# Operand sums of a seven-product gate/up projection made by accumulating transfers

## The chip, the cores and the metric

The kernel runs on one core of one Trainium2 chip. The metric is device time in microseconds of one launch. A core has a matrix engine (PE), a vector engine (DVE), an activation engine (ACT), a general engine (POOL) and a synchronisation engine (SP); SP, ACT and POOL each issue transfers on a queue of their own. Every engine works through its own instructions in order and waits on semaphores of the others.

## The reference, cut to what matters

One decoder layer serves 1024 prompt tokens and 8 sample tokens with the same weights, so all of the work below has T = 1032 columns (tokens). After attention, pooling and memory branches are merged into `h`, the layer ends so:

```python
    x = x + h @ w['w_out'][l]
    gate, up = jnp.split(rmsnorm(x, w['ffn_norm_g'][l]) @ w['w_gate_up'][l], 2, axis=-1)
    return x + (jax.nn.silu(gate) * up) @ w['w_down'][l]
```

D_MODEL is 1024, the hidden width is 2816 (22 tiles of 128), all data is float32.

## The kernel before, in words

Everything lies transposed: 128 features on the partitions, tokens along the row. Each float32 operand of a product is split into a rounded high part (a copy on ACT, `split`, line 239) and the remainder (a subtraction on DVE, line 240), and a product is three matmuls: high x high, high x low, low x high.

The end of the layer has three stages. First the output projection: for n = 0 to 7 a `gemm` fills four column chunks of 258 tokens, and `ev` adds the residual (L1323, DVE), stores it, scales it by the norm gain into `y` (L1325, ACT), squares it (L1329, ACT) and adds the square to `ssq2` (L1330, POOL). The tiles `y` are the activations, `hn[0..7]`. Write Y1 and Y2 for the first and second 516 tokens, and a (n < 4) and b (n from 4) for the two halves of the features. The stage also forms the activation operands of the seven products, among them sums and differences of Y1a, Y2a, Y1b, Y2b: `T1` at n < 4, and at n >= 4 a chain of three POOL operations, L1344 to L1346, each using the result of the one before.

The second stage is the gate/up projection by a seven-product scheme (Strassen's, in Winograd's form). Two weight tiles of 128 outputs, each cut into two halves of the features, make a 2 x 2 block matrix a11, a12, a21, a22. `wcombos` loads them (L1367, L1368), makes four sums on POOL (L1372 to L1376) and splits seven weight operands (`combo`, "combos" 0 to 6 here). The split combos take turns in six buffers, three tags of two. `strassen` then runs products 0 to 6; each is 24 matmuls, twelve for each 258-token half (`ps[0]` and `ps[1]`), in PSUM banks of tags s, t, g, p. Product 0 is copied out by ACT as `p1` (L1400) and product 2 is accumulated on top of it in the same banks, so product 2 waits for both copies. DVE adds the rest together, and POOL multiplies by the norm factor `rstd2` (L1415, L1423, L1428). One `wcombos` and one `strassen` are called a set here. There are 22 sets, gate and up in turn for 11 pairs of tiles. The third stage is the down projection.

The order of the instructions on each engine, within what dependences allow, is set when the program is built, by a scheduler that plans with estimated costs. Buffers come from pools of fixed counts: `wr` (raw weights) two, `tS` (sums) four.

Of the kernel before, what the change touches and what calls it, by code (L numbers as in the profile page):

```python
# [193 lines left out]
def body(nc, tc, xT, memT, w_p, w_m, w_v, w_mk, w_mv, w_up, w_un, w_out, w_gu, w_dn, w_pool, w_cmp, gains, consts, jlt,  # L194
# [37 lines left out]
    def gv(n, i=0):  # L232
        return gn[:, _GW[n][0] + i:_GW[n][0] + i + 1]
# [1074 lines left out]
    def opsplit(t, src, w):  # L1308
        split(src, t[:, :w], t[:, w:2 * w])
        return t  # L1310

    hn = [None] * 8
    ssq2 = rstd
    B11, B21, B22, T1, T2o, T3, T4n = ([None] * 4 for _ in range(7))
    for oi, n in enumerate(range(8)):
        wh, wl = wload(w_out[n], 1024)
        yt = hn[n] = T2(name="y")

        def ev(ci, c0, w, ps):
            xr = mg(w)  # L1320
            SY.dma_start(xr, xT[n][:, c0:c0 + w])
            x1 = tmp2(w, name="x1")
            V.tensor_add(x1, ps, xr)  # L1323
            SY.dma_start(x1d[n][:, c0:c0 + w], x1)
            S.activation(yt[:, c0:c0 + w], x1, AF.Copy, scale=gv("ffn", n))  # L1325
            if oi == 0:
                S.activation(ssq2[:, c0:c0 + w], x1, AF.Square)
            else:
                S.activation(x1, x1, AF.Square)  # L1329
                G.tensor_add(ssq2[:, c0:c0 + w], ssq2[:, c0:c0 + w], x1)  # L1330

        gemm(wh, wl, hh_, hl_, KD, ev, "t", CH4)

        y1, y2 = yt[:, :HT], yt[:, HT:]
        if n < 4:
            B11[n] = opsplit(T2(F32R, "b11"), y1, HT)
            t = sp.tile([128, HT], F32, name="tL", tag="L", bufs=2)
            G.tensor_sub(t, y2, y1)
# [16 lines left out]

    cc = [0]

    def combo(src, w=512):
# [3 lines left out]
        return opsplit(t, src, w)  # L1362

    def wcombos(s1, s2):

        r1, r2 = ([wp.tile([128, 1024], F32, name="wr", tag="wr", padded_shape=[128, T]) for _ in range(2)])
# [12 lines left out]

    def product(ps, a, b, first=True):  # L1380
# [11 lines left out]
    def strassen(w, z1, z2):  # L1392

        q = lambda h, c: slice(h * HT + c * HC, h * HT + c * HC + HC)
        px, pr = two("st"), two("gp")
        p1, u2 = [], []
        product(px, w[0], B11)
        for c in range(2):
            p1.append(tmp2(HC, "p1"))
            S.copy(p1[c], px[c])  # L1400
        product(pr, w[1], T1)
        product(px, w[2], B21, False)
        for c in range(2):
            V.tensor_mul(z1[:, q(0, c)], px[c], rstd2[:, q(0, c)])
        pq = two("st")
        product(pq, w[3], B22)
        py = two("st")
        product(py, w[4], T2o)
        for c in range(2):
            u2.append(mg(HC))  # L1410
            V.tensor_add(u2[c], py[c], p1[c])
            u4 = tmp2(HC, "u4")
            V.tensor_add(u4, pr[c], u2[c])
            V.tensor_add(z1[:, q(1, c)], pq[c], u4)
# [8 lines left out]
        G.tensor_mul(z2[:, HT:], z2[:, HT:], rstd2[:, HT:])  # L1423
# [77 lines left out]
```

## Time and profile before

| | |
|---|---|
| time, median of 3 runs | 1869.57 us (1867.78 to 1874.47) |
| profiled execution, its own time | 1869.54 us |
| span of its trace | 1867.8 us |
| PE busy | 96% of the span |
| DVE, ACT, POOL busy | 65%, 47%, 39% |

The profile is one execution. Its time is 1.7 us more than the span of its trace. Times in the views count from the span's start. An engine is counted as busy from the start to the end of each instruction, and matmuls overlap, so a busy PE is not by itself PE at its best rate; the number of matmuls in a stretch tells more.

### The profile page before, as it was taken

What the parts mean: (1) busy time and instruction counts of PE and PEld (TensorE: products, weight loads), DVE (VectorE), ACT (ScalarE), POOL (GpSimd) and SP (SyncE); (2) the same over time, 40 slices, a digit from 0 to 9 for tenths busy, and PEclk for the clock granted to TensorE, in tenths of its full rate; (3) what the DMA queues carried; (4) which work ended last, traced back from release to release, by engine and by line L of the source; (5) the groups of instructions that cost most, each with busy time, mean ns of one, the idle gap of its engine ahead of it and who ended that gap; (6) DMA issues with size and microseconds to landing.
All of it is one profiled execution on the core that took longest, in us unless ns stands there. A gap on an engine that the chain in (4) does not pass through costs nothing.

```text
span 1867.8 us, 34509 instructions
## 1 busy us (share of the span) xinstructions
PE 1798.3 (96%) x12337; PEld 1729.2 (93%) x12337; DVE 1210.0 (65%) x2748; ACT 870.7 (47%) x2012; POOL 737.5 (39%) x865
## 2 busy tenths in 40 slices
PE   6999999999999999989999999999999999999999
PEld 5998998888988999979989998899999999999999
DVE  8875788663564766778886834866666666636332
ACT  5643766445454676657774545422322223314100
POOL 5300211556341645457753437655545545100000
PEclk9999999899999999989999999999999999999999
DMA  4243124999665111552325643122222222546122
GB/s 162 100 148 139 65 101 164 296 316 315 205 201 169 53 43 63 179 165 78 108 64 177 213 134 100 62 87 78 71 80 80 84 87 69 170 131 184 59 69 94
DMA packets 142366, 241.13 MB, mean 129 GB/s; under 512 B 21449, under 2 KB 100450, under 8 KB 142194
## 3 DMA queue, kind: packets, MB, share of 16 engines
q1 hardware_dynamic: 118722, 189.69, 31.2%
q0 software_dynamic: 8496, 30.23, 4.8%
q10 hardware_dynamic: 14976, 19.01, 2.9%
q8 instruction: 97, 1.59, 0.4%
q14 instruction: 75, 0.61, 0.1%
HBM read 176.31 MB, written 62.55 MB: 128 GB/s over the span
## 4 chain that ended last, share of the span: by engine, by line
PE 55%; DMA 5%; DVE 4%; issue 2%; ACT 2%; POOL 1%; SPq 0%; ACTq 0%; DVEq 0%; POOLq 0%
PE ps_t L257 10%; PE ps_s L1385 10%; PE ps_t L1385 9%; PE ps_g L257 7%; PE ps_s L257 7%; PE ps_p L1061 3%; PE ps_s L1032 3%; PE ps_t L1077 2%; PE ps_g L1385 2%; PE ps_p L1385 2%; DMA mg<-acd 1%; DMA mg<-gd 1%; DMA gt<-gd 1%; DMA olr<-od 1%; DVE t L240 0%
## 5 line engine op out<-in xcount | busy, mean ns | idle before, releaser
L257 PE MATMUL ps_g<-xh,wh 128*128 128x344 f32 x624 | 206.1, 330 | 3.9 <-ACT mg L543 2.3
L257 PE MATMUL ps_g<-xl,wh 128*128 128x344 f32 x624 | 201.7, 323 | 0.0
L257 PE MATMUL ps_g<-xh,wl 128*128 128x344 f32 x624 | 201.6, 323 | 0.0
L239 ACT CAST wh<-wr 128x512 fp32r<-128x512 f32 (+3 forms) x138 | 99.9, 746 | 199.9 <-PE ps_t L257 83.5
L1051 POOL TENSOR_SCALAR P<-P,st,gate 128x384 f32<-128x384 f32 (+2 forms) x192 | 125.6, 664 | 94.6 <-DVE st L1046 37.8
L240 DVE TENSOR_TENSOR wl<-wr,wh 128x512 fp32r<-128x512 f32 (+3 forms) x112 | 105.0, 946 | 56.9 <-ACT wh L239 55.5
L239 ACT CAST cw<-tS 128x512 fp32r<-128x512 f32 x88 | 54.3, 619 | 182.0 <-PE ps_t L1385 98.2
L522 ACT ACTIVATE P<-P,st 128x384 f32<-128x384 f32 (+2 forms) x192 | 112.1, 586 | 40.1 <-DVE st L519 36.3
L257 PEld LDWEIGHTS ps_g<-xh,wh 128*128 128x128 f32 x624 | 118.2, 189 | 9.2 <-ACT mg L543 4.1
L257 PEld LDWEIGHTS ps_g<-xl,wh 128*128 128x128 f32 x624 | 118.5, 190 | 1.1 <-issue 0.4
L257 PEld LDWEIGHTS ps_g<-xh,wl 128*128 128x128 f32 x624 | 118.2, 189 | 1.3 <-issue 0.2
L240 DVE TENSOR_TENSOR ptl<-ps_t,pth 128x512 fp32r<-128x512 f32 (+1 forms) x208 | 108.0, 530 | 15.6 <-ACT pth L239 13.4
L239 ACT CAST pth<-ps_t 128x512 fp32r<-128x512 f32 (+1 forms) x208 | 91.3, 457 | 46.6 <-PE ps_t L1077 29.2
L240 DVE TENSOR_TENSOR cw<-tS,cw 128x512 fp32r<-128x512 f32 x88 | 93.3, 1061 | 29.7 <-ACT cw L239 26.1
L1385 PE MATMUL ps_s<-t,cw 128*128 128x258 f32 x792 | 106.1, 283 | 3.1 <-ACT rq L274 3.1
L1385 PE MATMUL ps_t<-t,cw 128*128 128x258 f32 x792 | 106.8, 283 | 2.1 <-DVE t L240 2.1
L1385 PE MATMUL ps_s<-b,cw 128*128 128x258 f32 x792 | 107.8, 286 | 0.0
L1385 PE MATMUL ps_t<-b,cw 128*128 128x258 f32 x792 | 105.6, 282 | 0.3 <-issue 0.3
L1385 PEld LDWEIGHTS ps_s<-t,cw 128*128 128x128 f32 x792 | 100.0, 190 | 3.3 <-ACT rq L274 3.3
L1385 PEld LDWEIGHTS ps_t<-t,cw 128*128 128x128 f32 x792 | 99.6, 189 | 2.9 <-DVE t L240 2.9
L1385 PEld LDWEIGHTS ps_s<-b,cw 128*128 128x128 f32 x792 | 101.4, 192 | 0.3
L519 DVE CUSTOM_DVE_ANT_0 P<-ps_s,ct 128x384 f32<-128x384 f32 (+3 forms) x160 | 83.2, 530 | 27.0 <-PE ps_t L1077 18.1
(527 smaller groups left out, 5659.0 us busy)
## 6 DMA issues: line engine op xcount, KB each, us to landing
kpg<-pg_k SPq DMA_DIRECT2D x128, 192.0 KB, 4.1
wr<-w_gu SPq DMA_DIRECT2D x44, 512.0 KB, 3.8
gd<-mg ACTq DMA_DIRECT2D x72, 172.0 KB, 3.4
wr<-w_m POOLq DMA_DIRECT2D x24, 512.0 KB, 5.4
acd<-zu SPq DMA_DIRECT2D x44, 258.0 KB, 2.0
mg<-acd SPq DMA_DIRECT2D x66, 172.0 KB, 3.0
mg<-gd SPq DMA_DIRECT2D x48, 172.0 KB, 2.4
wr<-w_p SPq DMA_DIRECT2D x16, 512.0 KB, 3.4
```

What stands on the lines that cost most here:

```text
L239: (he or S.copy)(hi, src)
L240: (le or V.tensor_sub)(lo, src, f(hi))
L257: PE.matmul(ps, lhsT=x, rhs=y, start=i == 0, stop=i == n - 1)
L519: V.tensor_tensor_reduce(P[u], s, m, -scale, ini, ALU.add, ALU.min, st[:, u:u + 1])
L522: S.activation(P[u], P[u], AF.Exp, bias=nm, scale=-1.0, accum_out=st[:, 6 + u:7 + u])
L1032: PE.matmul(ps, lhsT=u["q"][:, i * 128:i * 128 + 128], rhs=kk[:, k0 * 128 + a:k0 * 128 + a + n], start=x == 0, stop=x == 1)
L1051: lastp[:] = [G.tensor_scalar(p_, p_, st4[:, j, 5:6], gate[:, q, c:c + 1], op0=ALU.mult, op1=ALU.mult)]
L1061: PE.matmul(pv[:, c0:c0 + n], lhsT=lh, rhs=rhs, start=pvs["n"] == 0, stop=last, skip_group_check=True)
L1077: PE.transpose(pt_[:, x * 128:x * 128 + 128], pd[y][:, o - offs[y]:o - offs[y] + 128], ident)
L1385: PE.matmul(ps[c], lhsT=a[:, x * 512 + k * 128:x * 512 + k * 128 + 128], rhs=b[k][:, y * HT + c * HC:y * HT + c * HC + HC], start=first an ...
```

## The change

The sums of weights and the chain at n >= 4 are no longer computed on POOL. Each is a transfer that adds its source to its destination (`acc`), issued on POOL's queue, so POOL no longer computes in the last stages and only issues. A transfer can add but not subtract, so signs are moved: some activations are scaled by the negative gain (`ngn`), the raw tile r1 is negated in place on ACT (L1391 after), and some splits negate (`nsplit`). The weight tile's blocks are loaded several times, once into each sum's buffer. `x1` is one buffer that is added to three times and split between (combos 1, 3 and 4). The raw tile `wr` is now used once for each set, and `tS` has six buffers. Squares and the products with `rstd2` go to DVE, as do `T1` and all low parts. The products with `T2o` and `B22` change places.

```diff
+    def nsplit(src, hi, lo):
+        S.activation(hi, src, AF.Copy, scale=-1.0)
+        V.scalar_tensor_tensor(lo, src, -1.0, f(hi), op0=ALU.mult, op1=ALU.subtract)
+
+    def acc(dst, src):
+        G.dma_start(dst, src, accum_op=ALU.add)
...
-            S.activation(yt[:, c0:c0 + w], x1, AF.Copy, scale=gv("ffn", n))
+            S.activation(yt[:, c0:c0 + w], x1, AF.Copy,
+                         scale=gv("ffn", n) if (ci < 2) == (n < 4) else ngn[:, n:n + 1])
...
-                G.tensor_add(ssq2[:, c0:c0 + w], ssq2[:, c0:c0 + w], x1)
+                V.tensor_add(ssq2[:, c0:c0 + w], ssq2[:, c0:c0 + w], x1)
...
-            G.tensor_sub(x2, y2, x2)
-            G.tensor_add(x1, x1, x2)
-            G.tensor_sub(y1, y1, x1)
+            acc(x2, y2)
+            acc(x1, x2)
+            acc(y1, x1)
...
-        SY.dma_start(r1, s1)
-        SY.dma_start(r2, s2)
-        a11, a12, a21, a22 = r1[:, :512], r1[:, 512:], r2[:, :512], r2[:, 512:]
-        tS = lambda: sp.tile([128, 512], F32, name="tS", tag="S", bufs=4)
-        x1, x2, x3, x4 = tS(), tS(), tS(), tS()
-        G.tensor_add(x1, a21, a22)
-        r = [combo(a11), combo(x1), combo(a12)]
-        G.tensor_sub(x2, x1, a11)
-        G.tensor_sub(x4, a12, x2)
-        G.tensor_sub(x3, a11, a21)
-        r += [combo(x4), combo(x2), combo(x3), combo(a22)]
+        n11, n12 = r1[:, :512], r1[:, 512:]
+        SY.dma_start(r1, s1)
+        SY.dma_start(x1, s2[:, :512])
+        SY.dma_start(x3, s2[:, :512])
+        SY.dma_start(a22, s2[:, 512:])
+        acc(x1, s2[:, 512:])
+        S.activation(r1, r1, AF.Copy, scale=-1.0)
+        r = [combo(n11, True), combo(x1, True), combo(n12)]
+        acc(x1, n11)
+        acc(x3, n11)
+        r.append(combo(x1))
+        acc(x1, n12)
+        r += [combo(x1, True), combo(x3, True), combo(a22, True)]
...
-        G.tensor_mul(z1[:, HT:], z1[:, HT:], rstd2[:, HT:])
+        V.tensor_mul(z1[:, HT:], z1[:, HT:], rstd2[:, HT:])
...
-            split(src, t[:, :HT], t[:, HT:], le=G.tensor_sub if nm in ("t3", "t4") and k % 2 else None)
+            split(src, t[:, :HT], t[:, HT:])
```

POOL's queue before, at the end of the first stage (n = 7; `y_14234` is hn[3], `y_14816` hn[7], `wr` and `tS` those of the second set):

```order
L1344 TENSOR_TENSOR y_14234<-y_14816,y_14234 128x516
L1345 TENSOR_TENSOR y_14234<-y_14234 128x516
L1346 TENSOR_TENSOR y_14816<-y_14816,y_14234 128x516
L1330 TENSOR_TENSOR rstd_155<-rstd_155,x1_14943 128x258
L240 TENSOR_TENSOR t3_15078<-y_13940,t3_15078 128x516
L240 TENSOR_TENSOR t3_15084<-y_14234,t3_15084 128x516
L240 TENSOR_TENSOR t4_15090<-y_14526,t4_15090 128x516
L240 TENSOR_TENSOR t4_15096<-y_14816,t4_15096 128x516
L1372 TENSOR_TENSOR tS_15312<-wr_15309 128x512
```

The same place after (`y_14236` is hn[3], `y_14818` hn[7], `tS_15021` is x1 of the first set, `tS_15312` of the second):

```order
L1324 DMA tS_15021<-wr_15020 128x512
L1324 DMA y_14089<-y_14089 128x516
L1324 DMA y_14673<-y_14089 128x516
L1324 DMA y_14236<-y_14818 128x516
L1324 DMA tS_15021<-wr_15020 128x512
L1324 DMA y_14236<-y_14236 128x516
L1324 DMA y_14818<-y_14236 128x516
L1324 DMA tS_15560<-wr_15558 128x512
```

Computing instructions have become transfers, and a sum of the first set's weights now stands between the first and the second step of the last chain.

PE's queue before, around the first use of operands that need the chain (tiles b11, t1, b22 and t2 are activation operands, `rstd` with `ones` is the sum of squares over features):

```order
L1385 MATMUL ps_p_15104<-t1_14372,cw_15030 128x258 x3
L1385 MATMUL ps_t_15184<-b22_15051,cw_15039 128x258 x3
L1385 MATMUL ps_t_15184<-b22_15054,cw_15039 128x258 x3
L1385 MATMUL ps_t_15184<-b22_15057,cw_15039 128x258 x3
L1385 MATMUL ps_t_15184<-b22_15060,cw_15039 128x258 x3
L1385 MATMUL ps_t_15210<-t2_15063,cw_15042 128x258 x3
L1385 MATMUL ps_t_15210<-t2_15066,cw_15042 128x258 x3
L1385 MATMUL ps_t_15210<-t2_15069,cw_15042 128x258 x3
L1385 MATMUL ps_t_15210<-t2_15072,cw_15042 128x258
L1353 MATMUL ps_s_14986<-rstd_155,ones_141 128x258
L1385 MATMUL ps_s_15101<-b11_13926,cw_15027 128x258 x3
```

And after:

```order
L1405 MATMUL ps_t_15187<-t2_15054,cw_15041 128x258 x2
L1368 MATMUL ps_s_14988<-rstd_155,ones_141 128x258
L1405 MATMUL ps_s_15104<-b11_13928,cw_15030 128x258 x3
L1405 MATMUL ps_s_15104<-b11_14075,cw_15030 128x258 x3
L1405 MATMUL ps_s_15104<-b11_14222,cw_15030 128x258 x3
L1405 MATMUL ps_s_15104<-b11_14369,cw_15030 128x258 x3
L1405 MATMUL ps_t_15187<-t2_15054,cw_15041 128x258
L1405 MATMUL ps_t_15187<-t2_15057,cw_15041 128x258
L1405 MATMUL ps_s_15186<-t2_15054,cw_15041 128x258 x3
L1405 MATMUL ps_s_15186<-t2_15057,cw_15041 128x258 x3
L1405 MATMUL ps_s_15186<-t2_15060,cw_15041 128x258 x3
```

The T2o product, whose last tile needs two steps of the chain at n = 7, has moved ahead of the B22 product, which needs none, and product 2 (b21) has moved behind both.

ACT's queue before, for one gate or up set in the middle of the stage (weights of `wr_16050`, `wr_16051`):

```order
L239 CAST cw_16059<-wr_16050 128x512
L239 CAST cw_16062<-tS_16054 128x512
L239 CAST cw_16065<-wr_16050 128x512
L239 CAST cw_16071<-tS_16057 128x512
L239 CAST cw_16074<-tS_16055 128x512
L239 CAST cw_16077<-tS_16056 128x512
L1400 COPY p1_16121<-ps_s_16093 128x258
L239 CAST cw_16080<-wr_16051 128x512
L1400 COPY p1_16123<-ps_t_16094 128x258
```

And after, the set with `wr_16056` (`tS_16057` is x1, `wr_16554` the raw tile of the set after next):

```order
L1320 ACTIVATE cw_16066<-wr_16056 128x512
L1320 ACTIVATE cw_16069<-tS_16057 128x512
L239 CAST cw_16072<-wr_16056 128x512
L239 CAST cw_16077<-tS_16057 128x512
L1320 ACTIVATE cw_16081<-tS_16057 128x512
L1320 ACTIVATE cw_16084<-tS_16058 128x512
L1420 COPY p1_16128<-ps_s_16100 128x258
L1391 ACTIVATE wr_16554<-wr_16554 128x1024
L1320 ACTIVATE cw_16087<-tS_16059 128x512
L1420 COPY p1_16130<-ps_t_16101 128x258
```

Combos 1, 3 and 4 now read one buffer, and the negation of a later set's raw tile stands between the two copies of product 0.

## Rows read from the trace of the kernel before

**Rows 1.** The page, first part: busy time of each engine, its share, instructions.
```profile
PE 1798.3 (96%) x12337; PEld 1729.2 (93%) x12337; DVE 1210.0 (65%) x2748; ACT 870.7 (47%) x2012; POOL 737.5 (39%) x865
```

**Rows 2.** Windows in the seven-product stage; times x instructions, then granted clock, DMA share.
```profile
core 0: us, PE busy (x) PEld busy (x) DVE busy (x) ACT busy (x) POOL busy (x), PEclk, DMA share, GB/s
...
1200.00:1300.00 100.00, 100.00 (x839) 100.00 (x839) 67.84 (x116) 29.09 (x53) 53.67 (x36) 1.00 0.24 85
...
1500.00:1600.00 100.00, 100.00 (x839) 100.00 (x838) 64.71 (x112) 31.16 (x56) 52.72 (x35) 1.00 0.21 72
```

**Rows 3.** Timeline of PE, 1148 to 1200 us: start, duration, instruction, idle before it.
```profile
1156.48 0.28 PE L257 MATMUL ps_t<-mh,wl 128*128 128x258 f32 x1
...
1166.96 0.62 PE L1385 MATMUL ps_t<-t,cw 128*128 128x258 f32 x3 [0.90 <-DVE t L240]
...
1178.16 2.25 PE L1385 MATMUL ps_s<-t,cw 128*128 128x258 f32 x12 [3.12 <-ACT rq L274]
...
1189.94 1.62 PE L1385 MATMUL ps_s<-b,cw 128*128 128x258 f32 x12
```

**Rows 4.** Timeline of POOL, the last operand sums and splits ahead of the products.
```profile
1163.04 1.61 POOL L1344 TENSOR_TENSOR y<-y 128x516 f32<-128x516 f32 x1 [0.70 <-ACT y L1325]
...
1166.43 1.62 POOL L1346 TENSOR_TENSOR y<-y 128x516 f32<-128x516 f32 x1
...
1169.06 6.85 POOL L240 TENSOR_TENSOR t<-y,t 128x516 fp32r<-128x516 f32 x4
```

**Rows 5.** Timeline of DVE, then ACT, same stretch.
```profile
1168.86 7.60 DVE L240 TENSOR_TENSOR t<-y,t 128x516 fp32r<-128x516 f32 x5
...
1177.63 0.48 ACT L274 ACTIVATE rq<-ps_s,epst 128x258 f32<-128x258 f32 x1 [3.28 <-DVE rq L273]
```

**Rows 6.** Groups by line and form, 1190 to 1610 us: busy, mean ns, idle before.
```profile
L240 DVE TENSOR_TENSOR cw<-tS,cw 128x512 fp32r<-128x512 f32 x82 | 87.1, 1063 | 29.0 <-ACT cw L239 25.4 <-POOL zg L1428 3.2
...
L239 ACT CAST cw<-tS 128x512 fp32r<-128x512 f32 x81 | 50.2, 619 | 177.7 <-PE ps_t L1385 98.2 <-POOL tS L1372 66.9 <-POOL tS L1376 6.7
...
L1376 POOL TENSOR_TENSOR tS<-wr 128x512 f32<-128x512 f32 x20 | 34.9, 1745 | 0.0
...
L1450 DVE TENSOR_TENSOR zu<-zu,zg 128x516 f32<-128x516 f32 x41 | 28.5, 696 | 12.3 <-POOL zu L1428 11.9
...
L1413 DVE TENSOR_TENSOR u<-ps_g,mg 128x258 f32<-128x258 f32 x21 | 9.0, 427 | 0.7
...
L1400 ACT COPY p<-ps_s 128x258 f32<-128x258 f32 x21 | 7.8, 373 | 10.8 <-PE ps_s L1385 10.8
```

**Rows 7.** Tile wr and line L1285 (ns min/median/max); timeline of ACT, one cast of 1024 columns.
```profile
L240 DVE TENSOR_TENSOR cw<-wr,cw x61: 684/693/1781, 1195.1 to 1595.6; 128x512 fp32r<-128x512 f32 x61
...
L1285 DVE SCALAR_TENSOR_TENSOR ml<-acc,mh x24: 504/518/1244, 1021.9 to 1068.1; 128x344 fp32r<-128x344 f32 x24
...
1135.51 1.03 ACT L239 CAST wh<-wr 128x1024 fp32r<-128x1024 f32 x1
```

**Rows 8.** DMA issues: out<-in, queue, count, KB each, median us from issue to landing.
```profile
wr<-w_gu SPq DMA_DIRECT2D x44, 512.0 KB, 3.8
...
wr<-w_m POOLq DMA_DIRECT2D x24, 512.0 KB, 5.4
...
wr<-w_up POOLq DMA_DIRECT2D x8, 512.0 KB, 4.1
...
ol<-osp POOLq DMA_DIRECT2D x8, 256.0 KB, 2.4
...
ct<-consts POOLq DMA_DIRECT2D x1, 782.5 KB, 8.7
```

**Rows 9.** Line L244, instructions that issue a transfer on POOL: ns min/median/max.
```profile
L244 POOL DMA_DIRECT2D wr<-w_m x24: 538/557/610, 258.2 to 718.8; - x24
```

**Rows 10.** Timeline of PE, 1500 to 1521 us.
```profile
1500.05 1.62 PE L1385 MATMUL ps_s<-b,cw 128*128 128x258 f32 x12
...
1517.23 1.61 PE L1385 MATMUL ps_s<-b,cw 128*128 128x258 f32 x12
```

More of the change, by code (lines that the diff above doesn't have):

```diff
@@ L1310, in opsplit @@
         return t
+    ngn = sp.tile([128, 8], F32, name="ngn", tag="ngn", bufs=1)
+    V.tensor_scalar(ngn, gn[:, _GW["ffn"][0]:_GW["ffn"][0] + 8], -1.0, None, op0=ALU.mult)
+    def nsplit(src, hi, lo):
[3 more added lines that the diff above has]
+        G.dma_start(dst, src, accum_op=ALU.add)
     hn = [None] * 8
@@ L1336, in body @@
             B11[n] = opsplit(T2(F32R, "b11"), y1, HT)
-            t = sp.tile([128, HT], F32, name="tL", tag="L", bufs=2)
-            G.tensor_sub(t, y2, y1)
+            t = sp.tile([128, HT], F32, name="tL", tag="S", bufs=6)
+            V.tensor_add(t, y1, y2)
             T1[n] = opsplit(T2(F32R, "t1"), t, HT)
@@ L1356, in body, with combo @@
     cc = [0]
-    def combo(src, w=512):
+    def combo(src, neg=False):
         tag = ("wh", "wl", "wx")[cc[0] % 3]
@@ L1361, in combo @@
         t = (sp if tag == "wx" else wp).tile([128, 1024], F32R, name="cw", tag=tag, bufs=2)
-        return opsplit(t, src, w)
+        (nsplit if neg else split)(src, t[:, :512], t[:, 512:])
+        return t
     def wcombos(s1, s2):
-        r1, r2 = ([wp.tile([128, 1024], F32, name="wr", tag="wr", padded_shape=[128, T]) for _ in range(2)])
+        tS = lambda: sp.tile([128, HT], F32, name="tS", tag="S", bufs=6)[:, :512]
+        r1 = wp.tile([128, 1024], F32, name="wr", tag="wr", padded_shape=[128, T])
+        x1, x3, a22 = tS(), tS(), tS()
+        n11, n12 = r1[:, :512], r1[:, 512:]
         SY.dma_start(r1, s1)
-        SY.dma_start(r2, s2)
-        a11, a12, a21, a22 = r1[:, :512], r1[:, 512:], r2[:, :512], r2[:, 512:]
-        tS = lambda: sp.tile([128, 512], F32, name="tS", tag="S", bufs=4)
-        x1, x2, x3, x4 = tS(), tS(), tS(), tS()
-        G.tensor_add(x1, a21, a22)
-        r = [combo(a11), combo(x1), combo(a12)]
-        G.tensor_sub(x2, x1, a11)
-        G.tensor_sub(x4, a12, x2)
-        G.tensor_sub(x3, a11, a21)
-        r += [combo(x4), combo(x2), combo(x3), combo(a22)]
+        SY.dma_start(x1, s2[:, :512])
[9 more added lines that the diff above has]
+        r += [combo(x1, True), combo(x3, True), combo(a22, True)]
         return r
@@ L1404, in strassen @@
             V.tensor_mul(z1[:, q(0, c)], px[c], rstd2[:, q(0, c)])
-        pq = two("st")
-        product(pq, w[3], B22)
         py = two("st")
-        product(py, w[4], T2o)
+        product(py, w[3], T2o)
+        u4 = []
         for c in range(2):
@@ L1411, in strassen @@
             V.tensor_add(u2[c], py[c], p1[c])
-            u4 = tmp2(HC, "u4")
-            V.tensor_add(u4, pr[c], u2[c])
-            V.tensor_add(z1[:, q(1, c)], pq[c], u4)
-        G.tensor_mul(z1[:, HT:], z1[:, HT:], rstd2[:, HT:])
+            u4.append(tmp2(HC, "u4"))
+            V.tensor_add(u4[c], pr[c], u2[c])
+        pq = two("st")
+        product(pq, w[4], B22)
+        for c in range(2):
+            V.tensor_add(z1[:, q(1, c)], pq[c], u4[c])
+        V.tensor_mul(z1[:, HT:], z1[:, HT:], rstd2[:, HT:])
         pz = two("st")
@@ L1422, in strassen @@
             V.tensor_add(z2[:, q(1, c)], pr[c], u3[c])
-        G.tensor_mul(z2[:, HT:], z2[:, HT:], rstd2[:, HT:])
+        V.tensor_mul(z2[:, HT:], z2[:, HT:], rstd2[:, HT:])
         pw = two("st")
@@ L1427, in strassen @@
             V.tensor_add(z2[:, q(0, c)], pw[c], u3[c])
-        G.tensor_mul(z2[:, :HT], z2[:, :HT], rstd2[:, :HT])
+        V.tensor_mul(z2[:, :HT], z2[:, :HT], rstd2[:, :HT])
     acd = [dp.tile([128, T], F32, name=f"acd{i}") for i in range(NFF)]
     w = wcombos(w_gu[0], w_gu[1])
-    for o, nm, at, h in ((B22, "b22", 4, 1), (T2o, "t2", 0, 0), (T3, "t3", 0, 1), (T4n, "t4", 4, 0)):
+    for o, nm, at, h in ((T2o, "t2", 0, 0), (B22, "b22", 4, 1), (T3, "t3", 0, 1), (T4n, "t4", 4, 0)):
         for k in range(4):
             t, src = XG(nm), hn[at + k][:, h * HT:h * HT + HT]
-            split(src, t[:, :HT], t[:, HT:], le=G.tensor_sub if nm in ("t3", "t4") and k % 2 else None)
+            split(src, t[:, :HT], t[:, HT:])
             o[k] = t
```

## The prediction

> **What bounds the kernel now.** I read the page's first part, then the seven-product stage in windows, then the places where PE waits. PE is busy 96% of the span and every other engine at most 65% [rows 1], so only time in which PE stands still or runs slowly can be won. In the seven-product stage there is none: PE is busy for all of each window, at full granted clock, with 839 matmuls in 100 us [rows 2]. That is 0.1193 us for one matmul, 2.86 us for a product of 24 and 20.0 us for a set of seven. POOL is busy 53% there and DVE 65 to 68% [rows 2], and neither stops PE. So nothing that makes POOL or DVE cheaper in this stage can shorten it by itself.
>
> The place to win is the passage from the output projection to the first set. The last matmul of the projection starts at 1156.48 and lasts 0.28, so it ends at E = 1156.8; the second set starts at 1189.94 [rows 3]. The first set thus takes 33.2 us where its 168 matmuls need 20.0. Four sums of squares over the features lie between them, but most of the rest, some 11 to 12 us, is waiting. PE's timeline names the waits: DVE's split of an operand, then ACT's logarithm for the norm [rows 3]. ACT in turn waits 3.28 us for DVE [rows 5]. DVE is late because five of its splits take 7.60 us, or 1.5 each [rows 5], while POOL does four of its own in 6.85 [rows 4]; a split alone takes 0.69 [rows 7].
>
> **What the change removes.** On POOL, in each set four sums (the dearest 1.75 us [rows 6]) and three products, and ahead of the first set the chain, 1163.04 to 1168.05 for n = 7 [rows 4]. What POOL had cost DVE goes too: the split of a sum takes 1063 ns on average [rows 6] against a median of 693 for a split of raw weights [rows 7].
>
> **What it adds on DVE and ACT.** DVE gets three products of 516 columns in each set, at about 0.70 (L1450, same shape [rows 6]), together 2.1 us; four faster splits give back 4 x 0.37 = 1.5. The new form that negates and subtracts has the price of a plain subtraction: it took 518 ns for 344 columns [rows 7], and a straight line from 427 ns for 258 columns [rows 6] to 693 for 512 [rows 7] gives 517. DVE stays near 70%. ACT gets a negation of 1024 columns, 1.03 us [rows 7], and goes from 31% [rows 2] to 36%. The cover of both is PE's 20.0 us a set; neither becomes the bound.
>
> **What it adds on the transfers.** Four accumulating transfers in each set, 88 in all, and twelve for the activations. Their price D, from the moment the issue may start to the moment the next user may go on, is the unknown that decides. The trace has no accumulating transfer and none from SBUF to SBUF. The cheapest of POOL's queue with the same 256 KB takes 2.4 us; with 512 KB they take 4.1 and 5.4, with 782 KB 8.7 [rows 8]. An accumulating transfer reads its destination as well as its source, so it reads 512 KB, and I take the 512 KB row from the quieter stretch, D = 4.1, with 2.4 and 8.7 as the ends. The issue itself is 0.56 us of POOL [rows 9], hardly any load.
>
> **The first set, step by step.** After E, ACT still has a weight split (0.62 [rows 6]) and the last chunk of y (at most as much) to do, so y is ready at about E + 1.3. The T2o product needs hn[3] after two steps of the chain, one behind the other: E + 1.3 + 2D. Behind its split, ACT has, in the new order, four splits for B22, eight for T3 and T4 less one, and a weight: 13 casts at 0.62 are 8.1 us. Then come the copies of product 0 (0.37 [rows 6]), and product 2, T3 and T4 cannot start before them: 3 x 2.86 = 8.6. DVE's half of the same splits, 13 x 0.69, runs just behind and is covered. The second set starts at E + 1.3 + 2D + 8.1 + 0.4 + 8.6 = E + 18.4 + 2D. At D = 4.1 that is E + 26.6 against E + 33.2: 6.6 us won. The floor is the matmuls themselves, E + 20.0 and the four sums of squares; the gain is gone at D = 7.4. The other sum of the first set that stands in the chain's way on POOL's queue waits for a weight split that ends by E + 2.5, before the second step can start anyway.
>
> The Trainium skill, DMA: Bandwidth & Descriptors, Anatomy of one DMA, gives a transfer from POOL's queue as 2.0 us plus its bytes at 436 GB/s. That estimate is 3.2 us for 512 KB, and by it this passage would win 8.4 us and the whole would take 1861.1 us. The rows of 4.1 and 5.4 [rows 8] are slower than that estimate of the Trainium skill, and I follow the rows.
>
> **The later sets.** Here each set has a new chain, which must fit under PE. There are six buffers for seven split operands, so combo 1 of a set can be written when product 2 of the set before is done. In the trace, product 3 of a set starts at 1500.05 and product 2 of the next at 1517.23 [rows 10]: 17.2 us, six products. In that time x1 is split (0.62 + 0.69), added to (D), split again (1.31) and added to again (D). Only then is raw buffer r1 free; ACT's new order places the negation of the next load of that buffer between the two copies of product 0. So a load (3.8 [rows 8]), the negation (1.03), a split (0.62) and the copy (0.37) follow, and product 2's second half, which starts 1.43 later than the first, waits for the last of these. The chain is 2D + 8.4, to which I add two of DVE's evacuations queued ahead of the splits, 0.43 each [rows 6]: 2D + 9.3. The room is 17.2 + 1.4 = 18.6. At D = 4.1 the chain takes 17.5 and is hidden, with 1.1 us to spare; above D = 4.65 each set loses 2(D - 4.65), 21 times. What waits then is the copy p1 on ACT, and behind it PE.
>
> **The sum.** The profiled execution took 1869.54, which is the median of the three runs (1869.57), its span 1867.8 with 1.7 around it. 1869.5 - 6.6 + 0 = 1862.9, 0.4% less. I call anything within 0.5%, or 9.3 us, the same, about what a measurement of this kernel can tell from no change.
>
> **The rivals.**
> (1) Late operands: D is above 4.65 and every set stalls. For it speaks that POOL's 512 KB loads took 5.4 us in the busier stretch [rows 8], that the transfers per set rise from 1.3 MB to well over 2, and that the price of an accumulation is unseen; against it the quieter row of 4.1. At D = 5.4 the passage wins 33.2 - 29.2 = 4.0, and the sets lose 21 x 1.5 = 31.5: 1897. At the far end, D = 8.7, the passage loses 2.6 and the sets 21 x 8.1 = 170: 2042. It decides against the change by over 9.3 us from D = 4.65 + (9.3 + 5) / 42 = 5.0. Chance 0.35 for that.
> (2) A cheap transfer: D is near the 256 KB row, 2.4 [rows 8]. The first set then takes 23.2 us and 10.0 are won: 1859.5. To win over 9.3 us takes D below 2.75. For it speaks that the destination lies in SBUF and the row is the same size; against it the second read. Chance 0.15.
> (3) POOL cannot write its transfers' descriptors while DVE works. The issue takes 538 to 610 ns, in stretches where DVE was half busy [rows 9], and does not stretch, so little speaks for it. If each issue waited for two instructions of DVE (0.69 each), D would be 5.5 and the time 21 x 1.7 - 3.8 = 32 above, 1901. Chance 0.04. The Trainium skill, SBUF — State Buffer, Who interferes with whom, has such a lock for vector instructions that use both port pairs, and says that sums of two tensors are not among those that block the descriptors.
> (4) The passage is not shortened: another wait, the norm's logarithm or the copies queued on ACT behind the T2o split, keeps PE where it was, and the sets hide their chains. 1869, inside the forecast's class.
>
> **How the numbers follow.** Forecast, D from 2.75 to 4.65 with the sets hidden, 1860 to 1865: 0.36. Rival 4 and small stalls, D up to 5.0, 1865 to 1879: 0.10. Rival 2: 0.15. Rivals 1 and 3: 0.39. So faster by over 0.5% has 0.15, same 0.46, slower 0.39. The likeliest single case is the forecast, 1863, own range 1859 to 1867. The range for all goes from 1857, where the passage wins nearly the 13.2 us that the matmuls allow, to 1905, which takes in D up to about 5.6 and leaves out the dearest transfers, some 0.15.
>
> **What would show it.** Right: the accumulating transfers land 3.5 to 4.6 us after their issue; the second set starts about 27 us after the projection's last matmul; DVE's splits all take 0.69; PE has 838 matmuls in every 100 us of the later sets. Wrong: PE waits at product 2 in every set, with ACT's copy as the releaser and the negation waiting for a load, which is rival 1; a transfer that lands in time but is issued late behind another on POOL's queue; the first T2o product waiting beyond E + 12; or POOL's issues stretched above 0.7 us, which is rival 3.

## The result and the profile after

The changed kernel takes 1881.95 us (median of 7 runs, 1876.43 to 1886.02) against 1872.43 of the kernel before (7 runs, 1867.78 to 1874.47). The ratio is 1.0052, with a 95% interval of 1.0037 to 1.0067: slower, by 9.5 us at the medians. The profiled execution of the changed kernel took 1884.72 us, its span 1882.8.

First the windows of the changed kernel, as in [rows 2].

```profile
core 0: us, PE busy (x) PEld busy (x) DVE busy (x) ACT busy (x) POOL busy (x), PEclk, DMA share, GB/s
1200.00:1300.00 100.00, 96.73 (x793) 96.31 (x792) 62.96 (x123) 34.57 (x60) 17.57 (x20) 0.98 0.58 143
1500.00:1600.00 100.00, 100.00 (x837) 100.00 (x836) 67.06 (x131) 33.40 (x58) 15.80 (x18) 1.00 0.53 134
```

The later sets are as good as before (837 matmuls against 839), but the window from 1200 has 46 matmuls fewer. PE's waits from 1050 to 1640 us say where (us in total, times, the longest):

```profile
PE ps_t L257 <- DVE x L1337: 4.4, 5, 1.8
PE ps_t L1405 <- ACT p L1420: 2.8, 1, 2.8
PE ps_s L1405 <- ACT t L239: 2.5, 1, 2.5
```

L1337 is the evacuation of the output projection (the step that takes a finished chunk out of PSUM). The second row is one wait of the third set, the third the passage's. Before, PE waited 1.0 us for the evacuation there:

```profile
PE ps_t L257 <- DVE x L1323: 1.0, 2, 0.6
```

So the stretch is read in four parts. In the table, "projection" runs from the first matmul of the output projection to the end E of its last, "passage" from E to the start of the second set, then come the sets 2 to 5 (from the start of the second to the start of the fifth) and the rest to the end of the last matmul of the 22nd. All are read from PE's timeline as in [rows 3]; where the start of a set is split into pieces, it is that of its product 1 less 2.86. x3 is the buffer of the third weight operand; the kernels below are described with the experiments. The two profiles of before differ by 1.4 and 0.8 us in the first two columns, so smaller differences there say nothing. Each ratio is to runs of the kernel before that were taken together with that kernel.

| us, one profiled execution each | projection | passage | sets 2 to 5 | rest | time, median | ratio to before (95%) |
|---|---|---|---|---|---|---|
| before | 95.8 | 33.2 | 60.3 | 361.9 | 1872.43 | |
| before, a second profile | 94.4 | 32.4 | 60.3 | 361.9 | | |
| the change | 100.7 | 30.4 | 65.7 | 362.6 | 1881.95 | 1.0052 (1.0037 to 1.0067) |
| squares elsewhere | 96.2 | 29.3 | 63.5 | 362.4 | 1873.44 | 1.0011 (0.9998 to 1.0024) |
| squares on POOL | 103.4 | 34.4 | 65.7 | 362.7 | 1884.62 | 1.0072 (1.0045 to 1.0098) |
| no x3 sum (work left out) | 100.2 | 29.9 | 60.4 | 362.6 | 1874.35 | 1.0007 (0.999 to 1.0025) |
| weights only | 101.5 | 32.0 | 64.3 | 362.4 | 1881.36 | 1.0077 (1.0057 to 1.0097) |
| x3 last | 93.7 | 27.2 | 65.0 | 362.4 | 1866.17 | 0.9981 (0.9967 to 0.9996) |
| queues ordered | 94.2 | 25.0 | 65.1 | 362.4 | 1865.46 | 0.9976 (0.9964 to 0.9988) |
| x3 on DVE | 94.3 | 29.3 | 61.4 | 362.7 | 1865.75 | 0.9977 (0.9964 to 0.999) |
| x3 on POOL | 93.9 | 27.4 | 63.1 | 362.8 | 1865.92 | 0.9976 (0.9961 to 0.999) |
| last y first | 93.9 | 27.4 | 65.0 | 362.4 | 1867.34 | 0.998 (0.9968 to 0.9992) |
| ordered, no x3 (work left out) | 94.2 | 27.9 | 61.5 | 362.8 | 1866.21 | 0.9971 (0.9951 to 0.9991) |

Against the mean of the two profiles of before, the change loses 5.6 us in the projection, wins 2.4 in the passage, loses 5.4 in the sets 2 to 5 and 0.7 in the rest: 9.3, close to the 9.5 of the medians. The two profiled executions of before and after lie 15.2 apart; the other 6 us arose before the projection, where PE's instructions are the same. Its first matmul started at 1056.3 to 1067.6 us in the profiles of this study, 1061.0 and 1063.1 in the two of before, which lie inside that spread; so the table leaves such differences between executions out.

**The projection.** DVE, then ACT, then PE, near the end of the projection in the changed kernel:

```profile
1159.66 0.43 DVE L1345 TENSOR_TENSOR rstd<-rstd,x 128x258 f32<-128x258 f32 x1 [3.07 <-ACT x L1344]
1160.01 0.42 DVE L1337 TENSOR_TENSOR x<-ps_t,mg 128x258 f32<-128x258 f32 x1
...
1171.85 0.42 DVE L1337 TENSOR_TENSOR x<-ps_t,mg 128x258 f32<-128x258 f32 x1
```

```profile
1159.21 0.42 ACT L1344 ACTIVATE x<-x 128x258 f32<-128x258 f32 x1 [2.67 <-DMA x1d<-x]
...
1173.29 0.42 ACT L1344 ACTIVATE x<-x 128x258 f32<-128x258 f32 x1 [1.23 <-DMA x1d<-x]
...
1174.12 0.51 ACT L1339 ACTIVATE y<-x,gn 128x258 f32<-128x258 f32 x1
```

```profile
1160.48 0.39 PE L257 MATMUL ps_t<-mh,wh 128*128 128x258 f32 x1 [1.77 <-DVE x L1337]
```

The evacuation L1337 at 1160.01 stands behind the square sum L1345, which waited 3.07 us for ACT's square; the square is written over x1 and waited 2.67 us for the store of x1 to land. PE's next chunk starts at 1160.48 after 1.77 us of waiting. From 1067 to 1168 us DVE waited 38.3 us for the square. Before, POOL waited 33.4 us for it, and no evacuation stood behind POOL. The Trainium skill, Perfetto Trace Analysis, Tensor Engine Instruction, says that ACT, DVE and GpSimd are strict FIFO; this trace agrees, 3.07 us beside an evacuation whose matmuls were done.

**The passage.** PE and POOL:

```profile
1167.71 0.28 PE L257 MATMUL ps_t<-mh,wl 128*128 128x258 f32 x1
...
1182.78 0.58 PE L1405 MATMUL ps_s<-t,cw 128*128 128x258 f32 x1 [2.53 <-ACT t L239]
...
1198.41 1.62 PE L1405 MATMUL ps_s<-b,cw 128*128 128x258 f32 x12
```

```profile
1174.92 0.87 POOL L1324 DMA_DIRECT2D y<-y  x1 [5.21 <-ACT y L1339]
...
1178.57 0.87 POOL L1324 DMA_DIRECT2D y<-y  x1 [1.88 <-DMA y<-y]
```

E is 1168.0. The last y is ready at 1174.63, E + 6.6: in the rows above, its evacuation starts only at 1171.85, and on ACT the square of the chunk before it waits 1.23 us for its store, at 1173.29, ahead of this y. The two transfers are 3.65 us apart, and the cast follows at 1182.11.

**The third set.** POOL, ACT and PE:

```profile
1212.67 1.80 POOL L1324 DMA_DIRECT2D tS<-wr  x2 [8.75 <-DVE cw L240]
1219.27 0.87 POOL L1324 DMA_DIRECT2D tS<-wr  x1 [4.80 <-DVE cw L240]
```

```profile
1217.63 0.62 ACT L239 CAST cw<-tS 128x512 fp32r<-128x512 f32 x1 [5.80 <-DMA tS<-wr]
1223.47 1.15 ACT L1320 ACTIVATE cw<-tS 128x512 fp32r<-128x512 f32 x2 [5.22 <-DMA tS<-wr]
...
1227.54 1.06 ACT L1391 ACTIVATE wr<-wr 128x1024 f32<-128x1024 f32 x1 [2.66 <-DMA wr<-w_gu]
1229.02 0.35 ACT L1420 COPY p<-ps_t 128x258 f32<-128x258 f32 x1
```

```profile
1229.42 2.52 PE L1405 MATMUL ps_t<-b,cw 128*128 128x258 f32 x12 [2.79 <-ACT p L1420]
1231.74 2.35 PE L1405 MATMUL ps_s<-t,cw 128*128 128x258 f32 x12
1233.92 1.60 PE L1405 MATMUL ps_t<-t,cw 128*128 128x258 f32 x12
```

This is the chain that the prediction described for the later sets: sum, cast, sum, cast, load of the raw buffer, negation, copy, and PE waits for the copy. It happens once. After PE's wait of 2.79 us, twelve matmuls take 2.52 and 2.35 us instead of 1.60, so the wait costs about twice itself. In the program's order the two transfers issued at 1212.67 are the fourth set's x3 sum and the third set's first sum, in this order.

What comes late first can be read from the same trace, on POOL, SP and ACT:

```profile
1201.47 0.87 POOL L1324 DMA_DIRECT2D tS<-wr  x1 [5.10 <-DVE cw L240]
```

```profile
1205.04 0.33 SPq L1386 DMA_DIRECT2D wr<-w_gu  x1
```

```profile
1210.26 1.06 ACT L1391 ACTIVATE wr<-wr 128x1024 f32<-128x1024 f32 x1 [2.37 <-DMA wr<-w_gu]
```

By the program's order, the transfer of 1201.47 is the second set's second sum. It is issued 3.1 us behind the start of its set; in the sets from the fourth on, 2.8 to 3.5 us ahead of it. It reads the raw buffer, so the load of the fourth set's weights into that buffer is issued only at 1205.04, and their negation is done at 1211.3. The fourth set's x3 sum needs it, and the third set's first sum stands behind that sum on POOL's queue, though the split that it needs was done at 1209.0. So the third set's first sum is issued 5.3 us ahead of its set's start; from the fifth set on it is 9.0 to 9.6.

**The transfers.** Line L1324 (ns min/median/max of the issue; then us to landing), and the loads of SP, 1170 to 1640 us:

```profile
L1324 POOL DMA_DIRECT2D tS<-wr x63: 869/869/1261, 1175.5 to 1602.9; - x63
...
DMA to landing us min/median/max: 3.2/3.8/5.7
```

```profile
wr<-w_gu SPq DMA_DIRECT2D x20, 512.0 KB, 3.5
```

### The profile page after: what moved, and what is told of

Same layout as the page of the kernel before. It is cut to its first block, busy times and chain, and to the rows that moved or that the text cites. A ratio compares the mean times of both kernels' runs of the same rounds, so it can differ in the third digit from the quotient of the medians.

```text
span 1882.8 us, 34757 instructions
## 1 busy us (share of the span) xinstructions
PE 1807.9 (96%) x12337; PEld 1738.0 (92%) x12337; DVE 1214.3 (64%) x2851; ACT 890.2 (47%) x2034; POOL 541.6 (29%) x763
## 3 DMA queue, kind: packets, MB, share of 16 engines
q1 hardware_dynamic: 125058, 195.46, 32.4%
## 4 chain that ended last, share of the span: by engine, by line
PE 59%; DMA 11%; DVE 4%; issue 3%; ACT 3%; POOL 1%; SPq 1%; ACTq 0%; POOLq 0%; DVEq 0%
PE ps_g L257 9%; PE ps_t L1405 9%; PE ps_s L1405 9%; PE ps_t L257 7%; PE ps_s L257 6%; PE ps_p L257 4%; PE ps_p L1061 3%; DMA kpg<-pg_k 3%; PE ps_s L1032 3%; PE ps_t L1077 2%; PE ps_g L1405 1%; PE ps_p L1405 1%; DMA x1d<-x 1%; DMA mg<-acd 1%; DMA tS<-wr 1%
## 5 line engine op out<-in xcount | busy, mean ns | idle before, releaser
L1324 POOL DMA_DIRECT2D tS<-wr x66 | 61.6, 939 | 192.3 <-DVE cw L240 116.7
L1405 PEld LDWEIGHTS ps_t<-b,cw 128*128 128x128 f32 x792 | 101.4, 192 | 3.8 <-ACT p L1420 3.0
L1321 DVE SCALAR_TENSOR_TENSOR cw<-tS,cw 128x512 fp32r<-128x512 f32 x88 | 60.7, 689 | 67.1 <-ACT cw L1320 66.9
L1320 ACT ACTIVATE cw<-tS 128x512 fp32r<-128x512 f32 x88 | 53.1, 625 | 106.2 <-DMA tS<-wr 56.2
```

What stands on the lines that cost most here:

```text
L1320: S.activation(hi, src, AF.Copy, scale=-1.0)
L1321: V.scalar_tensor_tensor(lo, src, -1.0, f(hi), op0=ALU.mult, op1=ALU.subtract)
L1324: G.dma_start(dst, src, accum_op=ALU.add)
L1405: PE.matmul(ps[c], lhsT=a[:, x * 512 + k * 128:x * 512 + k * 128 + 128], rhs=b[k][:, y * HT + c * HC:y * HT + c * HC + HC], start=first an ...
```

## The experiments

The scheduler orders each kernel anew, so one changed line can move other instructions too. In the run without the x3 sum PE's order is unchanged and few others moved; with the squares elsewhere POOL's order is unchanged.

**Squares elsewhere.** The wait for the store is taken away by writing the square over the spent residual tile.

```diff
-                S.activation(x1, x1, AF.Square)
-                V.tensor_add(ssq2[:, c0:c0 + w], ssq2[:, c0:c0 + w], x1)
+                S.activation(xr, x1, AF.Square)
+                V.tensor_add(ssq2[:, c0:c0 + w], ssq2[:, c0:c0 + w], xr)
```

> The squares of the output projection are written over the spent residual tile instead of over x1, so that ACT's square no longer waits for the store of x1, and DVE's square sum no longer waits for that. Theory A (the wait for the store, passed on to DVE's evacuations): PE's waits on DVE's evacuation in the projection, 4.4 us in five waits in the changed kernel, fall under 1 us; the last matmul of the projection comes 4 to 5 us earlier; the operands are ready 1.5 to 3 us behind it instead of 6.8, and the second set starts 25.5 to 27.5 us behind it instead of 30.6. Time 7 to 10 us below the changed kernel's: 0.997 to 1.003 of the kernel before. Rival B (DVE is merely loaded with 28 more sums of 0.43 us): the waits on the evacuation stay above 3 us and the time within 3 us of the changed kernel's, 1.003 to 1.007 of before.

1873.44 us, 8.5 below the changed kernel: theory A, by the time and by the projection (96.2). The passage (29.3) and the waits on the evacuation (one of 1.96 us, not under 1) missed it. DVE, ACT and PE of this kernel show what is left:

```profile
1153.31 0.43 DVE L1345 TENSOR_TENSOR rstd<-rstd,mg 128x258 f32<-128x258 f32 x1 [6.20 <-ACT mg L1344]
```

```profile
1151.51 1.06 ACT L1391 ACTIVATE wr<-wr 128x1024 f32<-128x1024 f32 x1 [5.20 <-DMA wr<-w_gu]
...
1167.76 0.62 ACT L239 CAST t<-y 128x516 fp32r<-128x516 f32 x1 [3.16 <-DMA y<-y]
...
1168.81 0.51 ACT L1339 ACTIVATE y<-x,gn 128x258 f32<-128x258 f32 x1
```

```profile
1154.91 0.39 PE L257 MATMUL ps_t<-mh,wh 128*128 128x258 f32 x1 [1.96 <-DVE x L1337]
```

The one wait of 1.96 us now comes from another new instruction: the negation of the second set's raw weights waits 5.20 us on ACT for its load, the square stands behind it, and DVE behind the square. And the last y stands behind a cast that waits 3.16 us for a transfer, so it is ready at E + 5.5 and not at 1.5 to 3.

**Squares on POOL.**

```diff
-                V.tensor_add(ssq2[:, c0:c0 + w], ssq2[:, c0:c0 + w], x1)
+                G.tensor_add(ssq2[:, c0:c0 + w], ssq2[:, c0:c0 + w], x1)
```

> The square sums go back to POOL, nothing else. Theory A: the evacuations on DVE are free again, the last matmul of the projection comes 4 to 5 us earlier, as before the change. But POOL now waits for the store, with the accumulating transfers of the chain queued behind the square sums, so the passage to the second set stays at 28 to 31 us. Time 4 to 7 us below the changed kernel's: 1.000 to 1.003 of before. Rival B (late operands in all sets, price of the transfers): time as the changed kernel's, 1.004 to 1.007.

1884.62 us: theory A missed. The time is rival B's, but not for its reason, since the rest is that of the changed kernel (362.7 against 362.6). The evacuations still cost PE 4.5 us in three waits, and the passage grew to 34.4. With the sums off DVE, DVE waits for ACT's casts instead, and ACT still waits for the store and for the negation's load; PE, DVE and ACT, from 1060 us to E:

```profile
PE ps_t L257 <- DVE x L1337: 4.5, 3, 1.9
```

```profile
DVE b L240 <- ACT b L239: 20.9, 6, 7.3
```

```profile
ACT x L1344 <- DMA x1d<-x: 24.2, 11, 4.4
...
ACT wr L1391 <- DMA wr<-w_gu: 6.3, 2, 3.5
```

**No x3 sum.** The buffer x3 is split as combo 5.

```diff
         acc(x1, n11)
-        acc(x3, n11)
         r.append(combo(x1))
```

> Leaves out one accumulating transfer in each set, the one that adds the raw weights to the third operand (that sum is missing from the result). Theory A (the third set's 5.5 us come from the second operand's sum standing behind this transfer on POOL's queue and sharing its engines): the cast after the first sum comes 3.6 instead of 5.0 us behind its issue, and the third set's waits of 0.5 and 2.8 us on the copy of product 0 shrink by 1 us or go; 2 to 6 us below the changed kernel. Rival B (the third set is late because its load of raw weights is issued late): those waits stay, and the time falls by less than 1.5 us. Rival C (every set pays): matmuls per 100 us rise from 835 to 837 to 839 and the time falls by 3 us or more spread over the sets.

1874.35 us, 7.6 below the changed kernel, and PE has no wait in the third set: theory A, though with more than the 2 to 6 us that it gave; 5.3 of them are in the sets 2 to 5. The rest did not change, against rival C. The third set's first sum is now issued 9.2 us ahead of its set, which starts at 1213.0:

```profile
1203.74 0.87 POOL L1324 DMA_DIRECT2D tS<-wr  x1 [5.29 <-DVE cw L1321]
```

**Weights only.** The activations' chain and the square sums are POOL's instructions again.

```diff
-            acc(x2, y2)
-            acc(x1, x2)
-            acc(y1, x1)
+            G.tensor_add(x2, x2, y2)
+            G.tensor_add(x1, x1, x2)
+            G.tensor_add(y1, y1, x1)
```

> The activations' sums and the square sums go back to POOL; only the weights' sums are made by transfers. Theory A (the loss at the output projection and the gain in the passage both belong to the activations' part, the third set's stall to the weights'): the evacuations wait under 2 us, the second set starts 32 to 35 us behind the projection's last matmul as before the change, the third set still stalls by about 5 us; 1.003 to 1.006 of before. Rival B (the weights' transfers and the negations, queued in the projection ahead of POOL's and ACT's work, are what delays the evacuations): the evacuations still wait 3 us or more, and the time is 1.006 to 1.010 of before, as with the squares on POOL.

1881.36 us: rival B. The passage is as before, and the third set stalls, as theory A had it; but the projection still takes 101.5. PE's longest wait there, 4.18 us, follows from the negation: the cast for which DVE's split waits stands behind it on ACT, and the evacuation stands behind that split. ACT and DVE:

```profile
1141.69 1.06 ACT L1391 ACTIVATE wr<-wr 128x1024 f32<-128x1024 f32 x1 [3.98 <-DMA wr<-w_gu]
```

```profile
1144.15 2.92 DVE L240 TENSOR_TENSOR b<-y,b 128x516 fp32r<-128x516 f32 x1 [8.73 <-ACT b L239]
1146.99 0.74 DVE L1337 TENSOR_TENSOR x<-ps_t,mg 128x258 f32<-128x258 f32 x2
```

**x3 last**, on top of the squares elsewhere (`issue_after(i)` queues what it holds behind i on the same engine).

```diff
         acc(x1, n11)
-        acc(x3, n11)
         r.append(combo(x1))
-        acc(x1, n12)
+        d = acc(x1, n12)
+        with tc.issue_after(d.ins):
+            acc(x3, n11)
```

> On top of the squares written elsewhere, the transfer that adds the raw weights to the third operand is queued on POOL behind both sums of the second operand, in every set; the result is the reference's. Theory A (the third set stalls because the second operand's sum stands behind that transfer and lands 5.8 instead of about 4 us after the cast was due): the waits on the copy of product 0 in the third set, 2.9 us, go, and the stretch from the second to the fifth set takes 62 us instead of 65.2; time 2.5 to 4 us below the kernel with the squares elsewhere, 0.998 to 1.000 of before. Rival B (the load of raw weights is late): nothing changes there and the time stays within 1 us, 1.000 to 1.002. Rival C (the third operand now comes late for product 5): new waits of PE in every set, slower by 10 us or more.

1866.17 us, 0.9981 of before, and neither theory: the stall stayed (65.0, with a wait of 2.89 us), while projection and passage became 2.5 and 2.1 us shorter, with another order on POOL's queue there too. PE no longer waits for an evacuation, though the second set's negation still waits 4.83 us for its load ahead of the squares. The place of that transfer in the queue alone is not the stall.

**Queues ordered**, on top of that. The lines of the three moves (`ly[0]` is the last y, `mid[0]` the y of the second chunk of n = 7):

```diff
+            with tc.issue_after(ly[0].ins):
+                split(src, t[:, :HT], t[:, HT:])
...
+    with tc.issue_after(d.ins):
+        for y1, x1 in last:
+            acc(y1, x1)
...
+        with (tc.issue_after(after.ins) if after else nullcontext()):
+            S.activation(r1, r1, AF.Copy, scale=-1.0)
```

> As the run before it, and three more changes of order alone: ACT's casts of the summed activations stand behind its last y, the third step of the chain for n = 6 stands behind the second step for n = 7 on POOL, and the negation of the second set's raw weights stands two chunks later on ACT. Theory A (what is lost against the forecast is only that ready work stands behind waiting work in the queues): y is ready 1.5 to 2.5 us behind the last matmul of the projection instead of 5.5, the second set starts 25.5 to 27 us behind it instead of 29.3, and PE's one wait of 2.0 us on the evacuation shrinks; time 4 to 7 us below the squares-elsewhere kernel by this and 2.5 to 4 by the third set: 1862 to 1867, 0.995 to 0.998 of before. Rival B (the passage is bound elsewhere, by the norm's logarithm or the casts): the second set still starts 28.5 to 30 us behind, time 1868 to 1871.

1865.46 us, 0.9976 of before, the fastest median of the series. The projection costs 94.2, as before the change, and the passage is 25.0 us, half a microsecond below what theory A gave. ACT and PE:

```profile
1156.66 0.51 ACT L1340 ACTIVATE y<-x,gn 128x258 f32<-128x258 f32 x1
...
1165.39 0.62 ACT L239 CAST t<-y 128x516 fp32r<-128x516 f32 x1 [0.60 <-DMA y<-y]
```

```profile
1181.18 1.62 PE L1416 MATMUL ps_s<-b,cw 128*128 128x258 f32 x12
...
1210.18 2.47 PE L1416 MATMUL ps_s<-b,cw 128*128 128x258 f32 x12 [2.96 <-ACT p L1431]
```

With E at 1156.2, y is ready at E + 1.0 and the second set starts at E + 25.0. The third set still stalls, and gives back 4.8 us.

**Sum twice**, on the kernel with x3 last.

```diff
         acc(x1, n11)
+        acc(x1, n11)
```

> As the kernel with the third operand's transfer last, but the first raw sum of the second operand is made twice in every set, so that a wrong multiple of those weights is in the result: one more accumulating transfer in the chain of each set. Theory A (the room of 18.6 us is nearly used up, the chain being 2D + 9.3 = 16.7 with D = 3.7): the chain becomes 3D + 9.3 = 20.4, and each set waits 1.5 to 3 us for the copy of product 0: 30 to 60 us above the kernel without it. Rival B (there is much more room than was reckoned): no more than 5 us above it.

1926.23 us (2 runs), 60 above the kernel without it: theory A. PE waits in nearly every set for the copy of product 0 (1250 to 1640 us; no such row in the changed kernel):

```profile
PE ps_s L1407 <- ACT p L1422: 24.1, 16, 2.8
PE ps_t L1407 <- ACT p L1422: 10.0, 10, 1.4
```

A set takes 22.9 us (from the copies at 1264.43 and 1631.03, sixteen sets) instead of 20.1.

**x3 on DVE and x3 on POOL**, each on the ordered kernel; the diff is that of the first.

```diff
-        d = acc(x1, n12)
-        with tc.issue_after(d.ins):
-            acc(x3, n11)
+        acc(x1, n12)
+        V.tensor_add(x3, x3, n11)
```

> As the kernel with the ordered queues, but the third operand's sum is made by DVE in each set instead of by a transfer; the result is the reference's. Theory A (what is left of the third set's stall, 4.8 us in the stretch from the second to the fifth set, comes from transfers that collide and queue there: the first sum landed 6.9 us after its issue with the transfer engines over nine tenths busy): the stretch takes 60.3 to 61.5 us instead of 65.1, as in the run that left that transfer out; time 3.5 to 5 us below the ordered kernel, 0.993 to 0.996 of before. Rival B (the third set's chain is too long from the moment its split may be written, with or without that transfer): the stretch still takes 64 us or more, and the time is within 1 us of the ordered kernel's. Rival C (DVE, with 0.7 us more in every set and the wait for the negation, holds back the evacuations): new waits in the later sets, slower than the ordered kernel.

> The same with POOL as the engine that makes the third operand's sum. By theory A the stretch from the second to the fifth set is 60.3 to 62 us too, if it is the transfer's traffic; if it is its place in POOL's queue, ahead of the second operand's sums and waiting for a negation, the stall stays, 63 to 66 us, since POOL's sum stands in that queue as well. DVE's casts beside POOL's sum take up to 1 us instead of 0.69, in every set, and are hidden. Time 0.993 to 0.998 of before.

By the stretch, theory A for DVE, 61.4. On POOL it is 63.1, just inside what was expected if the sum's place in POOL's queue counts. But the times are those of the ordered kernel, 1865.75 and 1865.92, since the passage went back to 29.3 and 27.4. With the sum on DVE the reason is again an order: the last y, at 1157.43, came behind a weight split that waited 3.56 us.

**Last y first** puts that split behind the last y:

```diff
-        r.append(combo(x1))
+        with (tc.issue_after(ly[0].ins) if first else nullcontext()):
+            r.append(combo(x1))
```

> As the kernel with the third operand's sum on DVE, where the last y stood on ACT behind a weight split that waited 3.56 us for PE, and so came 3.8 us behind the projection instead of 1.0; here that split stands behind the last y. If the formula for the passage holds (y ready, two transfers, thirteen casts, copies, three products), the second set starts 25 to 26.5 us behind the projection's last matmul instead of 29.4, the stretch from the second to the fifth set stays at 61 to 62 us, and the time is 2.5 to 4 us below: 1861 to 1864, 0.994 to 0.997 of before. If the passage is bound elsewhere, 28 us or more and the time unchanged, 0.997 to 0.999.

A miss: 1867.34 us. The passage is 27.4, not 25 to 26.5 (PE then waits 1.5 us for the norm's logarithm), and the stall of the third set is back, 65.0, though no transfer makes the third operand's sum. ACT of this kernel, then of the kernel with x3 on DVE, shows the difference:

```profile
1211.51 0.36 ACT L1431 COPY p<-ps_s 128x258 f32<-128x258 f32 x1
1216.42 1.06 ACT L1401 ACTIVATE wr<-wr 128x1024 f32<-128x1024 f32 x1 [4.56 <-DMA wr<-w_gu]
...
1217.90 0.35 ACT L1431 COPY p<-ps_t 128x258 f32<-128x258 f32 x1
```

```profile
1206.53 0.36 ACT L1430 COPY p<-ps_s 128x258 f32<-128x258 f32 x1
...
1207.31 0.36 ACT L1430 COPY p<-ps_t 128x258 f32<-128x258 f32 x1
1212.14 1.06 ACT L1401 ACTIVATE wr<-wr 128x1024 f32<-128x1024 f32 x1 [4.46 <-DMA wr<-w_gu]
```

Where the negation, which waits 4.5 us for its load, stands between the two copies, PE waits for the second copy; where it stands behind both, PE does not. The two kernels differ in more places than this one, so the negation's place is seen beside the stall and not shown to be its cause.

**Ordered, without the x3 sum.** The ordered kernel with the transfer left out as above.

> The kernel with the ordered queues, without the transfer that adds the raw weights to the third operand (that sum is missing from the result). In every kernel of this series that ends with the reference's result, the projection's end to the start of the fifth set took 90.2 us or more, however early the second set began: what the passage won, the third set gave back. Theory A (the third operand's transfer is what delays the third set, also when the passage is short): the stretch from the second to the fifth set takes 60.3 to 61.5 us, and with a passage of 25 to 27 us the whole 85.5 to 88. Theory B (the third set's own chain of two sums, counted from the projection's end, bounds it, and it only met a slow passage in the earlier run without that transfer): the whole stays at 89.5 us or more, with a stall of 3 us or more in the third set.

Inconclusive: the stall is 1.2 us (61.5), but the passage came out at 27.9, since the last y again stood behind a split that waited 3.67 us, and the two together take 89.4. That E to the fifth set can be 85.5 to 88 was not shown.

## Why the prediction was wrong

The forecast of 1863 was wrong and the sign with it. That the range held the time is luck: its upper part was there for a stall in every later set (rivals 1 and 3), and no such stall came. By its steps:

- **"What it adds on DVE and ACT"** is the step that failed. It priced what each set adds by its duration and named PE's 20 us a set as the cover. The 28 square sums that go to DVE in the projection, and the two negations that fall there, are not in it: their cost was put at nothing without a reason. It did not ask what the square sum waits for and what stands behind it on DVE. The square sum brought the wait for the store ahead of the evacuations, and the negation brought the wait for a load ahead of the squares and casts. Cost: 5.6 us in the projection. That the wait for the store is most of it is shown: without it 4.5 of the 5.6 came back. The rest, 1.1 us, is less than the two profiles of before differ by; it came back with x3 last, where a negation still stood there. So what the negation costs is seen in single waits of PE (1.96 us in one kernel, 4.18 in another), but no run takes it away by itself. That DVE's sums alone are the cause is refuted by the run with the squares on POOL.
- **"y is ready at about E + 1.3"** failed for a reason of the same kind, work ahead of the last evacuation and the last y in DVE's and ACT's queues, some of it waiting: E + 6.6, or 5.3 us late. Without the wait for the store it was still E + 5.5. The passage fell only 3.8 short of its forecast (30.4 against 26.6), because other terms were too high: the two transfers took 7.2 instead of 8.2, the thirteen casts 7.2 instead of 8.1. The formula was right: in the ordered kernel y came at E + 1.0 and the second set at E + 25.0. One reading ahead of it was not: PE's waits in the passage of before come to 6.3 us, not 11 to 12. Another part of that time went into matmuls at a lower granted clock, 0.72 on average from 1178 to 1184 us, with 35 matmuls in these 6 us.
- **D.** Taken at 4.1; the transfers of the chain stood 3.65 us apart, and the median from issue to landing is 3.8. By the Trainium skill, DMA: Bandwidth & Descriptors, Anatomy of one DMA, 256 KB are estimated at 2.6 us and 512 KB at 3.2; the median in this trace is above both.
- **The later sets** are hidden, as forecast. The sum made twice lengthened each set by 2.8 us, so by the formula 3D + 9.3 is 21.4 and D there 4.0: of the room of 18.6 the real chain leaves 1.2 us, near the 1.1 foreseen.
- **The third set** was counted among the later ones, and cost 5.4 us once. It is rival 1's chain in a single set: with 1.2 us to spare, it breaks where a sum or a load lands later than in the steady state. In the changed kernel the lateness starts in the second set, whose second sum comes about 6 us later against its set's start than in the later sets, and reaches the third set through a load, a negation and the fourth set's x3 sum. The cast waited 5.80 us for the first sum, which was "issued late behind another on POOL's queue", as the prediction's own list of signs had it. That in the changed kernel the stall hangs on the transfer of the x3 sum is shown (60.4 without it, 65.7 with it). The negation between the copies is only seen beside the stall (65.0 against 61.4). Neither is the cause in every order: the stall stayed with that transfer queued last, and came back without it. What delays the third set in the other orders was not separated further.
- **The floor.** E to the start of the fifth set took 93.5 and 92.7 us before, 96.1 to 100.0 in the three kernels with all sums made and the square still over x1, 98.0 with the sum made twice, and 89.4 to 92.9 in all others. What a shorter passage won, the third set mostly gave back. Why it does not fall below 89 stays open.
- **Rival 3's sign** appeared without its cause: the issue takes 0.87 us, above 0.7, but its median is 869 to 877 ns in every group of transfers, against a least value of 862 and a greatest of 1261, so it is its ordinary length here and no wait for DVE is seen in it.

## What to carry to other kernels

An instruction that moves to another engine takes its waits with it. Before its duration is priced, list what it waits for and what stands behind it in the new queue: POOL could wait 33 us here at no cost to PE; on DVE, 38 us of the same waits cost PE 4.4. And a chain that just fits in the steady state should be reckoned once more for the first two rounds, where a late operand of one set delays the loads, and through the queues the sums, of the next two.

## What was not expected of the hardware

An accumulating transfer occupies POOL for 0.87 us where a plain one took 0.56 [rows 9]. Accumulating transfers whose source is the weights in memory (`tS<-w_gu` on POOL's queue) took 5.4 us at the median to land, against 3.8 for those from SBUF with the same 256 KB. And a stop of 2.8 to 3.0 us of PE was followed by two groups of twelve matmuls at 2.35 to 2.52 us instead of 1.60, so that each such stop cost nearly 5 us; in the ordered kernel the granted clock was 0.66 of the full 2.4 GHz on average from 1210 to 1215 us, so part of it went by at the lower of the two levels, 1.2 GHz.
